# The last rows of a matmul with row normalization: a square moved from ScalarE to VectorE, and scalings moved to GpSimd

## The chip, the core and the metric

The kernel runs on one core of a Trainium2 chip. The metric is the device time of one execution in microseconds (us). A profiled execution leaves a trace as well: start and duration of every instruction on TensorE (PE), VectorE (DVE), ScalarE (ACT) and GpSimd (POOL), and the issues and landings of the transfers that SyncE's queue (SP) starts.

## The reference

```python
x = np.matmul(a, b)                                   # 2048 x 2048 by 2048 x 2048, fp32
rms = np.sqrt(np.mean(x ** 2, axis=-1, keepdims=True) + eps)
return (gamma * x / rms).astype(np.float32)           # gamma: one value per column
```

A row can be written only when the squares of all of its 2048 columns are summed. What follows that sum is one factor r = 1/rms per row, which is a column of 128 values, one per partition, for a block of 128 rows.

## The kernel before

The output has 16 blocks of 128 rows. Blocks are worked on in pairs (`g`), and each pair in two halves of 1024 columns (`j`), by a Strassen-like scheme of seven products on 512-column chunks: `do(n, m)` issues the eight matmuls of product `m` of half `n` (`product`, line 363, matmul at line 358), and the chunks x11, x12, x21, x22 are put together from PSUM banks by additions on VectorE (`add`, line 101) and copies on ScalarE. In a half, x11 and x12 are the 512-column chunks of the pair's first block, x21 and x22 those of its second. The kernel writes every engine's order by hand: each engine runs its instructions in the order of the program's text, and waits come from the dependences alone.

The change lies in the last function, `last_group`, which finishes the last pair of blocks: `ra` is block 14, `rb` is block 15. For `rb`, four chunks of 512 columns are squared and summed into the columns of a small tile `msq[rb]` (`square_of`, line 272, an ACT Square whose accumulator output is the sum). The steps that the prediction speaks of are these.

- Line 814: ACT copies the bank of the last product 7 to x21[1].
- Lines 818 to 822 scale three chunks of block 14 by its factor `r_a`: ACT the left one (`by_r`, line 754), POOL the chunk `mid` (line 820), DVE x11[1] (line 822). The fourth, x12[1], gets gamma and `r_a` in one DVE instruction (`scaled_gamma`, line 750, called at line 826). SP writes them out in three transfers (lines 819, 821, 827: 256, 256 and 512 KB).
- Lines 823 to 825: DVE adds the x21[1] of line 814 to two half banks of 256 columns each, and to x22[1].
- Line 828 is the last full product. Its result is the left chunk of block 15; ACT squares it (line 829) straight from PSUM, then squares x22[1] (line 830), and DVE multiplies the left chunk by gamma (line 831).
- Lines 832 and 845: two small DVE instructions put together `part`, the sum of all squares of block 15 but for those of the very last 256 columns.
- Lines 837 to 846: the last product goes in two halves of 256 columns (matmuls at line 839), each squared by ACT (line 842). Between the two, DVE makes `part` and multiplies the chunk x22[1] by gamma (line 846).
- Line 847: ACT takes the root (line 288), DVE the reciprocal `r_b` (line 293).
- Lines 848 to 854 scale block 15: DVE the left chunk (line 848), then SP writes it (line 849, 256 KB); ACT chunks 1 and 3 (line 851, recorded as line 754), DVE chunk 2 in two halves with gamma (line 853, recorded as line 750). SP's last transfer (line 854, 768 KB) waits for all three.

Of the kernel before, what the change touches and what calls it, by code (L numbers as in the profile page):

```python
# [8 lines left out]
FP32 = mybir.dt.float32  # L9
# [4 lines left out]
ALU = mybir.AluOpType  # L14
# [3 lines left out]
def kernel(  # L18
# [13 lines left out]
    nc = tc.nc  # L32
    P = 128
# [6 lines left out]
    CH = 512  # L40
# [13 lines left out]
    stat_pool = ctx.enter_context(tc.tile_pool(name="stat_pool", bufs=4))  # L54
# [3 lines left out]
    inv_sqrt_n = 1.0 / float(N) ** 0.5  # L58
# [41 lines left out]
    def add(out, in0, in1, op=ALU.add):  # L100
        nc.vector.tensor_tensor(out=out, in0=in0, in1=in1, op=op)  # L101
# [104 lines left out]
    msq = {}  # L206
# [53 lines left out]
    def x_tile(mb, h):  # L260
        if (mb, h) not in x_half:
            x_half[mb, h] = x_slot[slot_of[mb, h]]
        return x_half[mb, h]

    def x_chunk(mb, c):
        return x_tile(mb, c // 2)[:, (c % 2) * CH:(c % 2 + 1) * CH]

    def square_of(mb, src):
        c = n_sq[mb]
        n_sq[mb] += 1  # L270
        sq = sq_pool.tile([P, 2 * CH], BF16, name="sq")
        nc.scalar.activation(out=sq[:, 0:src.shape[-1]], in_=src, func=ACTF.Square,  # L272
                             scale=inv_sqrt_n, accum_out=msq[mb][:, c:c + 1])

    def square_half(mb, h):
        square_of(mb, x_tile(mb, h))
# [4 lines left out]
    def take_pre(mb):  # L281

        pre_of[mb] = stat_pool.tile([P, 1], FP32, name="pre")
        add(pre_of[mb], msq[mb][:, 0:1], msq[mb][:, 1:2])
# [11 lines left out]
    def square_right(mb):  # L296

        square_half(mb, 1)
        rms_of[mb] = root(msq[mb][:, 2:3], pre_of.pop(mb))

    def rows(mb, lo, hi):
        return out[mb * P:(mb + 1) * P, lo:hi]
# [207 lines left out]
    x11, x12, x21, x22 = (x_chunk(r, c) for r in (r2, r3) for c in (2, 3))  # L510
# [45 lines left out]
    def chunks(n):  # L556
        g, j = halves[n]
        return [x_chunk(2 * g + r, 2 * j + c) for r in range(2) for c in range(2)]

    def do(n, m, copies=True):  # L560

        if n >= len(halves) or n < 0:
            return
        g, j = halves[n]
        b1, b2, b3 = B1[n % 2], B2[n % 2], B3[n % 2]
        if g >= G2:
            b1 = b2
        product(g, j, m, {1: b1, 2: b1, 3: b3, 4: b2, 5: b3, 6: b2, 7: B7}[m],
                start=m in (1, 7))
        if m == 1 and g >= G2:  # L570
            nc.scalar.copy(out=chunks(n)[0], in_=b2)
        elif m == 1:
            nc.scalar.copy(out=b2, in_=b1)  # L573
        elif m == 6:
            nc.scalar.copy(out=b3, in_=b2)  # L575
        elif m == 7 and copies:
            nc.scalar.copy(out=chunks(n)[2], in_=B7)  # L577
# [44 lines left out]
    def first_sums(n):  # L622

        return [chunks(m)[0] for m in (n - 2, n - 1, n, n + 1)]
# [115 lines left out]
    def last_group():  # L740
        n = len(halves) - 2
        g = NG - 1
        ra, rb = 2 * g, 2 * g + 1
        x11, x12, x21, x22 = zip(chunks(n), chunks(n + 1))
        xa, xb = x_tile(ra, 0), x_tile(rb, 0)
        gam = [gamma_sb[:, c * CH:(c + 1) * CH] for c in range(NCH)]
        gam_left = gamma_sb[:, 0:HALF]

        def scaled_gamma(x, src, r, gamma_of_x):
            nc.vector.scalar_tensor_tensor(out=x, in0=src, scalar=r, in1=gamma_of_x,  # L750
                                           op0=ALU.mult, op1=ALU.mult)

        def by_r(x, r):
            nc.scalar.activation(out=x, in_=x, func=ACTF.Copy, scale=r)

        b2, b3 = [B2[(n + j) % 2] for j in range(2)], [B3[(n + j) % 2] for j in range(2)]
        x00, x01 = first_sums(n)[0:2]
        do(n, 6)
        step(g - 1, 1, X2)
        nc.scalar.copy(out=W2, in_=X2)  # L760
        square_right(rb - 2)
        do(n - 1, 3)
        step(g - 1, 2, W2)
        step(g - 1, 6, X2)
        nc.scalar.copy(out=Y2, in_=X2)
        finish(rb - 2)
        take(n - 1, 12)
        add(x00, W2, x00)
        do(n + 1, 1)
        step(g - 1, 5, Y2)  # L770
        step(g - 1, 7, W2)
        step(g - 1, 4, X2)
        square_half(ra - 2, 0)
        add(x11[1], Y2, x11[1])
        a_sums(g, (4,))
        add(x11[0], W2, x11[0])
        add(x11[1], W2, x11[1])
        take_pre(ra - 2)
        square_of(ra, x11[1])
        do(n, 5)  # L780
        nc.scalar.copy(out=x22[0], in_=b3[0])
        add(x11[0], X2, x11[0])
        step(g - 1, 3, Y2)
        add(x01, Y2, x01)
        square_right(ra - 2)
        do(n + 1, 6)
        finish(ra - 2)
        do(n, 7)
        add(x22[0], x21[0], x22[0])
        add(b2[0], b2[0], x21[0])  # L790
        square_of(rb, x22[0])
        add(x11[1], x11[1], gam[2], ALU.mult)
        do(n + 1, 5)
        nc.scalar.copy(out=x22[1], in_=b3[1])
        wide = a_pool.tile([P, K], FP32, name="a32")
        chunk = [wide[:, c * CH:(c + 1) * CH] for c in range(NCH)]
        add(chunk[1], x22[0], gam[1], ALU.mult)
        pre_b = stat_pool.tile([P, 1], FP32, name="part")
        add(pre_b, msq[rb][:, 0:1], msq[rb][:, 1:2])
        do(n, 3)  # L800
        take(n, 12)
        square_half(ra, 0)
        pre_a = stat_pool.tile([P, 1], FP32, name="pre")
        nc.vector.tensor_scalar(out=pre_a, in0=msq[ra][:, 0:1], scalar1=msq[ra][:, 1:2],
                                scalar2=msq[ra][:, 2:3], op0=ALU.add, op1=ALU.add)
        add(xa, xa, gam_left, ALU.mult)
        do(n + 1, 3)
        take(n + 1, 12)
        square_of(ra, x12[1])
        rms_a = root(msq[ra][:, 3:4], pre_a)  # L810
        r_a = inverse(rms_a)
        other = X2
        product(g, 1, 7, other)
        nc.scalar.copy(out=x21[1], in_=other)
        halves2 = [slice(0, CH // 2), slice(CH // 2, CH)]
        half = [bank[:, 0:CH // 2] for bank in (B1[1], b3[0])]
        left, mid = xa[:, 0:CH], xa[:, CH:]
        by_r(left, r_a)
        nc.sync.dma_start(out=rows(ra, 0, CH), in_=left)
        nc.gpsimd.tensor_scalar_mul(out=mid, in0=mid, scalar1=r_a)  # L820
        nc.sync.dma_start(out=rows(ra, CH, HALF), in_=mid)
        nc.vector.tensor_scalar_mul(out=x11[1], in0=x11[1], scalar1=r_a)
        for bank, col in zip(half, halves2):
            add(bank, b2[1][:, col], x21[1][:, col])
        add(x22[1], x21[1], x22[1])
        scaled_gamma(x12[1], x12[1], r_a, gam[3])
        nc.sync.dma_start(out=rows(ra, HALF, N), in_=x_tile(ra, 1))
        do(n, 4)
        square_of(rb, b2[0])
        square_of(rb, x22[1])  # L830
        add(xb[:, 0:CH], b2[0], gam[0], ALU.mult)
        nc.vector.tensor_scalar(out=pre_b, in0=pre_b, scalar1=msq[rb][:, 2:3],
                                scalar2=msq[rb][:, 3:4], op0=ALU.add, op1=ALU.add)

        half_sq = stat_pool.tile([P, 2], FP32, name="n2")
        part = stat_pool.tile([P, 1], FP32, name="part")
        for h, (bank, col) in enumerate(zip(half, halves2)):
            for kp in range(KP):
                nc.tensor.matmul(bank, quarter(g, 1, 1)[:, kp, :], sums[1][:, 2, kp, col],
                                 start=False, stop=(kp == KP - 1), skip_group_check=True)  # L840
            sq = sq_pool.tile([P, 2 * CH], BF16, name="sq")
            nc.scalar.activation(out=sq[:, 0:CH // 2], in_=bank, func=ACTF.Square,
                                 scale=inv_sqrt_n, accum_out=half_sq[:, h:h + 1])
            if h == 0:
                add(part, half_sq[:, 0:1], pre_b)
                add(chunk[3], x22[1], gam[3], ALU.mult)
        r_b = inverse(root(half_sq[:, 1:2], part))
        nc.vector.tensor_scalar_mul(out=xb[:, 0:CH], in0=xb[:, 0:CH], scalar1=r_b)
        nc.sync.dma_start(out=rows(rb, 0, CH), in_=xb[:, 0:CH])
        for c in (1, 3):  # L850
            by_r(chunk[c], r_b)
        for bank, col in zip(half, halves2):
            scaled_gamma(chunk[2][:, col], bank, r_b, gam[2][:, col])
        nc.sync.dma_start(out=rows(rb, CH, N), in_=wide[:, CH:])

    first_segment()
# [37 lines left out]
```

## Time and profile before

| | us |
|---|---|
| median of three runs | 220.34 |
| lowest and highest of them | 219.80, 221.61 |
| the profiled execution, its own time | 219.88 |
| its span in the trace | 218.10 |
| PE busy in the span | 207.6 (95%) |
| DVE busy | 161.9 (74%) |
| ACT busy | 113.6 (52%) |
| POOL busy | 36.8 (17%) |
| last matmul issued, its start | 210.85 |
| last transfer issued | 213.83 |

The profiled execution took 1.78 us more than its span and lies 0.46 us below the median of the three runs. A line of the timeline gives start, duration, engine, line of the program, operation, and output and inputs with their shapes. An idle time before an instruction and what ended it stand in square brackets. SPq is the queue from which SyncE issues transfers.

### The profile page before, as it was taken

The page shows a single profiled execution, that of the slowest core. Times are in us where ns is not written, and L with a number is a line of the kernel's source. Part 1 is how long each engine was busy: PE and PEld are TensorE (multiplying, and loading weights), DVE is VectorE, ACT ScalarE, POOL GpSimd, SP SyncE. Part 2 cuts the span into 40 slices and gives each one's busy share as a digit, 9 for nine tenths or more (in the row PEclk, how much of TensorE's full clock was granted, in tenths as well). Part 3 has the DMA queues.
Part 4 walks back from the last instruction along what each step waited for, and adds up shares of the span by engine and source line. Part 5 has one row for each costly group of instructions (what it writes and reads, how often), then busy time and mean ns, then how long its engine had stood idle before and what let it go on. Part 6 is the DMA issues. An engine that isn't in the chain of part 4 may idle for free.

```text
span 218.1 us, 2969 instructions
## 1 busy us (share of the span) xinstructions
PE 207.6 (95%) x1004; PEld 97.1 (45%) x1024; DVE 161.9 (74%) x327; ACT 113.6 (52%) x225; POOL 36.8 (17%) x73
## 2 busy tenths in 40 slices
PE   7899999999999999999999999999999999999970
PEld 3444544444455444444444444444444444444440
DVE  1128769999999974989985899399856984485781
ACT  2110002900598565889726962594728951555782
POOL 7544444334001000300021001100101000000030
PEclk9999999999999999999999999999999999999996
DMA  7999999999949888599774995497595993040454
GB/s 153 171 201 207 203 206 209 212 207 221 408 171 377 304 228 238 150 345 283 237 227 168 345 277 100 183 243 241 126 273 215 316 256 72 0 192 3 192 187 198
DMA packets 37039, 46.60 MB, mean 214 GB/s; under 512 B 22560, under 2 KB 26656, under 8 KB 35744
## 3 DMA queue, kind: packets, MB, share of 16 engines
q0 software_dynamic: 10608, 23.86, 45.3%
q1 hardware_dynamic: 26144, 22.29, 34.8%
q10 hardware_dynamic: 272, 0.26, 0.3%
q8 instruction: 8, 0.13, 0.2%
q14 instruction: 7, 0.06, 0.1%
HBM read 34.60 MB, written 16.78 MB: 236 GB/s over the span
## 4 chain that ended last, share of the span: by engine, by line
PE 80%; DMA 6%; ACT 6%; DVE 4%; issue 2%; POOL 1%; ACTq 0%; another core or an unknown queue 0%; SPq 0%; POOLq 0%
PE acc L358 53%; PE acc L406 16%; PE acc L397 3%; DMA early<-in_a_dram 3%; DMA out_dram<-x 3%; ACT sq L272 2%; PE tbank L397 2%; PE tbank L432 2%; DVE x L311 2%; PE tbank L182 2%; PE tbank L358 1%; DVE x L101 1%; ACT acc L573 0%; PE tbank L195 0%; POOL b L115 0%
## 5 line engine op out<-in xcount | busy, mean ns | idle before, releaser
L358 PEld LDWEIGHTS <-s 128*128 128x128 f16 (+1 forms) x312 | 30.4, 98 | 37.5 <-DVE s L335 1.1
L272 ACT ACTIVATE sq<-x 128x1024 bf16<-128x1024 f32 (+1 forms) x33 | 33.2, 1005 | 25.0 <-DVE x L101 21.1
L406 PE MATMUL acc<-b,head_at 128*128 128x512 bf16 x171 | 42.3, 379 | 0.6 <-DMA b<-in_b_dram 0.4
L311 DVE SCALAR_TENSOR_TENSOR x<-x,r,gamma_sb 128x1024 f32<-128x1024 f32 x28 | 34.9, 1282 | 0.5
L358 PE MATMUL acc<-b,head_at 128*128 128x512 bf16 x133 | 33.6, 379 | 0.2
L101 DVE TENSOR_TENSOR x<-acc,x 128x512 f32<-128x512 f32 x33 | 22.2, 687 | 10.7 <-PE acc L397 4.7
L358 PEld LDWEIGHTS <-head_at 128*128 128x128 f16 (+1 forms) x184 | 17.9, 98 | 21.0
L358 PE MATMUL acc<-b,at_even 128*128 128x512 bf16 x110 | 26.2, 379 | 0.2
L406 PEld LDWEIGHTS <-head_at 128*128 128x128 bf16 x176 | 16.9, 97 | 19.7 <-issue 0.7
L358 PE MATMUL acc<-early,s 128*128 128x512 bf16 x102 | 25.4, 379 | 0.2
L358 PE MATMUL acc<-b,s 128*128 128x512 bf16 x100 | 24.3, 379 | 0.2
L358 PEld LDWEIGHTS <-at_even 128*128 128x128 f16 x160 | 15.7, 98 | 18.9
L224 ACT ACTIVATE sq<-a 128x1024 bf16<-128x1024 f32 x22 | 23.3, 1058 | 0.5
L358 PE MATMUL acc<-t_left,s 128*128 128x512 bf16 x95 | 22.5, 379 | 0.1
L115 POOL DMA_DIRECT2D b<-in_b_dram x32 | 17.2, 541 | 20.5 <-DMA b<-in_b_dram 14.1
L442 ACT COPY x<-acc 128x512 f32<-128x512 f32 x7 | 4.1, 580 | 25.6 <-PE acc L406 25.6
L575 ACT COPY acc<-acc 128x512 f32<-128x512 f32 x12 | 6.9, 575 | 10.6 <-PE acc L358 10.6
L293 DVE RECIPROCAL r<-rms 128x1 f32<-128x1 f32 x16 | 2.6, 160 | 12.1 <-ACT rms L288 12.0
L187 DVE COPY head_at<-tbank 128x1024 bf16<-128x1024 bf16 x7 | 4.8, 692 | 8.3 <-PE tbank L182 8.3
L820 POOL TENSOR_SCALAR x<-x,r 128x512 f32<-128x512 f32 x1 | 1.9, 1855 | 42.0 <-DVE r L293 42.0
L101 DVE TENSOR_TENSOR x<-tbank,x 128x512 f32<-128x512 f32 x9 | 6.2, 689 | 3.6 <-PE tbank L432 3.6
L577 ACT COPY x<-acc 128x512 f32<-128x512 f32 x10 | 5.8, 585 | 5.0 <-PE acc L358 5.0
(133 smaller groups left out, 244.7 us busy)
## 6 DMA issues: line engine op xcount, KB each, us to landing
out_dram<-x SPq DMA_DIRECT2D x29, 512.0 KB, 3.7
a<-in_a_dram POOLq DMA_DIRECT2D x9, 1024.0 KB, 5.9
b<-in_b_dram POOLq DMA_DIRECT2D x32, 256.0 KB, 9.9
a<-in_a_dram POOLq DMA_DIRECT2D x4, 512.0 KB, 9.8
early<-in_a_dram POOLq DMA_DIRECT2D x7, 256.0 KB, 10.0
gamma_sb<-in_gamma_dram POOLq DMA_DIRECT2D x2, 512.0 KB, 9.9
head_at<-in_a_dram POOLq DMA_DIRECT2D x1, 1024.0 KB, 8.9
out_dram<-x SPq DMA_DIRECT2D x3, 256.0 KB, 2.6
```

The lines of the kernel that those rows point to most:

```text
L101: nc.vector.tensor_tensor(out=out, in0=in0, in1=in1, op=op)
L115: nc.gpsimd.dma_start(out=raw[j][kp][:, t, :], in_=b[lo:lo + P, j * HALF:(j + 1) * HALF])
L182: nc.tensor.matmul(view[:, t, r, :], ah(kp)[:, r, t * P:(t + 1) * P], identity, is_transpose=True, start=(t == 0 and r == 0), stop=(t == 1 ...
L187: nc.vector.tensor_copy(out=head_at[:, 2 * kp:2 * kp + 2, :, :], in_=view)
L224: nc.scalar.activation(out=junk, in_=a32[mb][:, h * HALF:(h + 1) * HALF], func=ACTF.Square, scale=2.0 ** -8, accum_out=n2[:, h:h + 1])
L272: nc.scalar.activation(out=sq[:, 0:src.shape[-1]], in_=src, func=ACTF.Square, scale=inv_sqrt_n, accum_out=msq[mb][:, c:c + 1])
L311: nc.vector.scalar_tensor_tensor(out=x, in0=x, scalar=inverse_of[mb], in1=gamma_sb[:, h * HALF:(h + 1) * HALF], op0=ALU.mult, op1=ALU.mult)
L358: nc.tensor.matmul(bank, lhsT[:, kp, :], rhs, start=(start and kp == 0), stop=(kp == KP - 1), skip_group_check=not start)
L397: nc.tensor.matmul(bank, lhsT[:, k, :], rhs, start=(m in (1, 7) and k == 0), stop=(k == KQ - 1), skip_group_check=m not in (1, 7))
L406: nc.tensor.matmul(bank, head_at[:, kt, r, :], head_rhs(c, kt), start=(kt == 0), stop=(kt == KT - 1))
L575: nc.scalar.copy(out=b3, in_=b2)
L577: nc.scalar.copy(out=chunks(n)[2], in_=B7)
```

## The change

VectorE computes the squares of x22[1] and their sum itself, in one `tensor_tensor_reduce` that writes the squares into the not yet used `chunk[3]` and starts its sum from `pre_b`; it stands before the scaling of x12[1]. The ACT square of x22[1] and the small DVE instruction of line 832 are gone, and `part` is made by one instruction with three summands. In block 14, x11[1] is scaled by GpSimd instead of VectorE, behind `mid`. In block 15, ACT scales the left chunk (before: VectorE), GpSimd chunk 1 (before: ACT), and chunk 3 is shared, its first 256 columns by ACT and its last 256 by GpSimd (before: all by ACT, 512 columns). Every scaling on GpSimd is now a `tensor_scalar` with two multiplications, by r and by 1.0.

```diff
+        def by_r_pool(x, r):
+            nc.gpsimd.tensor_scalar(out=x, in0=x, scalar1=r, scalar2=1.0,
+                                    op0=ALU.mult, op1=ALU.mult)
+
         by_r(left, r_a)
         nc.sync.dma_start(out=rows(ra, 0, CH), in_=left)
-        nc.gpsimd.tensor_scalar_mul(out=mid, in0=mid, scalar1=r_a)
+        by_r_pool(mid, r_a)
         nc.sync.dma_start(out=rows(ra, CH, HALF), in_=mid)
-        nc.vector.tensor_scalar_mul(out=x11[1], in0=x11[1], scalar1=r_a)
+        by_r_pool(x11[1], r_a)
         for bank, col in zip(half, halves2):
             add(bank, b2[1][:, col], x21[1][:, col])
         add(x22[1], x21[1], x22[1])
+        sum_b = stat_pool.tile([P, 1], FP32, name="sum_b")
+        nc.vector.tensor_tensor_reduce(out=chunk[3], in0=x22[1], in1=x22[1],
+                                       scale=inv_sqrt_n * inv_sqrt_n, scalar=pre_b,
+                                       op0=ALU.mult, op1=ALU.add, accum_out=sum_b)
         scaled_gamma(x12[1], x12[1], r_a, gam[3])
         nc.sync.dma_start(out=rows(ra, HALF, N), in_=x_tile(ra, 1))
         do(n, 4)
         square_of(rb, b2[0])
-        square_of(rb, x22[1])
         add(xb[:, 0:CH], b2[0], gam[0], ALU.mult)
-        nc.vector.tensor_scalar(out=pre_b, in0=pre_b, scalar1=msq[rb][:, 2:3],
-                                scalar2=msq[rb][:, 3:4], op0=ALU.add, op1=ALU.add)
...
             if h == 0:
-                add(part, half_sq[:, 0:1], pre_b)
+                nc.vector.tensor_scalar(out=part, in0=half_sq[:, 0:1], scalar1=msq[rb][:, 2:3],
+                                        scalar2=sum_b, op0=ALU.add, op1=ALU.add)
                 add(chunk[3], x22[1], gam[3], ALU.mult)
         r_b = inverse(root(half_sq[:, 1:2], part))
-        nc.vector.tensor_scalar_mul(out=xb[:, 0:CH], in0=xb[:, 0:CH], scalar1=r_b)
+        by_r(xb[:, 0:CH], r_b)
         nc.sync.dma_start(out=rows(rb, 0, CH), in_=xb[:, 0:CH])
-        for c in (1, 3):
-            by_r(chunk[c], r_b)
+        by_r_pool(chunk[1], r_b)
         for bank, col in zip(half, halves2):
             scaled_gamma(chunk[2][:, col], bank, r_b, gam[2][:, col])
+        by_r(chunk[3][:, halves2[0]], r_b)
+        by_r_pool(chunk[3][:, halves2[1]], r_b)
         nc.sync.dma_start(out=rows(rb, CH, N), in_=wide[:, CH:])
```

## The prediction

> **What bounds the kernel now.** I read the page first: PE is busy for 95% of the span, but all edits lie behind line 818, and the last matmul starts at 210.85 of 218.1 us. So only the tail counts. There the chain that ended last runs (ACT copy 207.68, ACT by_r, a wait for the product of line 828 until 209.41, four ACT squares, root, reciprocal, two ACT scalings, the last transfer). Then I read the timeline of the last 11 us, engine by engine.
>
> ```profile
> 207.68 0.59 ACT L814 COPY x<-tbank 128x512 f32<-128x512 f32 x1
> 207.86 0.49 DVE L822 TENSOR_SCALAR x<-x,r 128x512 f32<-128x512 f32 x1
> 207.92 1.85 POOL L820 TENSOR_SCALAR x<-x,r 128x512 f32<-128x512 f32 x1 [42.02 <-DVE r L293]
> 208.30 0.76 DVE L101 TENSOR_TENSOR acc<-acc,x 128x256 f32<-128x256 f32 x2
> 208.97 0.68 DVE L101 TENSOR_TENSOR x<-x 128x512 f32<-128x512 f32 x1
> 209.57 0.75 DVE L750 SCALAR_TENSOR_TENSOR x<-x,r,gamma_sb 128x512 f32<-128x512 f32 x1
> 210.13 0.63 ACT L272 ACTIVATE sq<-x 128x512 bf16<-128x512 f32 x1
> 210.24 0.68 DVE L101 TENSOR_TENSOR x<-acc,gamma_sb 128x512 f32<-128x512 f32 x1
> 210.88 0.38 ACT L842 ACTIVATE sq<-acc 128x256 bf16<-128x256 f32 x1
> 210.89 0.27 DVE L832 TENSOR_SCALAR part<-part,msq 128x1 f32<-128x1 f32 x1
> 211.39 0.38 ACT L842 ACTIVATE sq<-acc 128x256 bf16<-128x256 f32 x1
> 211.39 0.16 DVE L101 TENSOR_TENSOR part<-n,part 128x1 f32<-128x1 f32 x1 [0.23 <-ACT sq L842]
> 211.47 0.68 DVE L101 TENSOR_TENSOR a<-x,gamma_sb 128x512 f32<-128x512 f32 x1
> 211.90 0.30 ACT L288 ACTIVATE rms<-n,part 128x1 f32<-128x1 f32 x1
> 212.23 0.16 DVE L293 RECIPROCAL r<-rms 128x1 f32<-128x1 f32 x1
> 212.43 0.49 DVE L848 TENSOR_SCALAR x<-x,r 128x512 f32<-128x512 f32 x1
> 212.47 1.33 ACT L754 ACTIVATE a<-a,r 128x512 f32<-128x512 f32 x2 [0.28 <-DVE r L293]
> 212.94 0.33 SPq L849 DMA_DIRECT2D out_dram<-x  x1
> 213.83 0.33 SPq L854 DMA_DIRECT2D out_dram<-a  x1
> ```
>
> The reader is to see two things. ACT sets r_b: its squares follow one another without a gap until the root at 211.90. But DVE is only just behind: it waited 0.23 us before `part`, and the multiplication of line 846 ended at 211.47 + 0.68 = 212.15, 0.08 before the reciprocal of 212.23. DVE has some 0.3 us of slack in this stretch, no more.
>
> Two more views. One is POOL beside DVE at line 146, where POOL copies a single column; the other is the list of transfers, with the median from issue to landing as its last number.
>
> ```profile
> 87.58 1.25 POOL L146 CAST pace<-head_at 128x1 f32<-128x1 f16 x1 [19.55 <-DMA head_at<-a]
> ...
> 87.50 2.48 DVE L311 SCALAR_TENSOR_TENSOR x<-x,r,gamma_sb 128x1024 f32<-128x1024 f32 x2
> ...
> 164.82 0.19 POOL L146 COPY pace<-a 128x1 f32<-128x1 f32 x1 [7.24 <-DMA a<-in_a_dram]
> ```
>
> ```profile
> out_dram<-x SPq DMA_DIRECT2D x3, 256.0 KB, 2.6
> out_dram<-a SPq DMA_DIRECT2D x1, 768.0 KB, 3.3
> ```
>
> The POOL copy of one column takes 0.19 us beside an idle DVE, and a POOL cast of one column took 1.25 us when it began during a two-input DVE instruction: it ended at 88.83, where the first of the two DVE instructions ended (87.50 + 1.24 = 88.74). So a POOL row contains time in which POOL only waited for DVE.
>
> **The change part by part.**
>
> *ScalarE loses the square of line 830* (210.13 to 210.86, with its accumulator read: 0.75 us). This isn't gained in full, for PE is late next. The last matmul runs 210.85 to 211.12; from the last matmul of line 828 (ends about 209.2) to the ACT square that needs it (209.41) passed 0.2 us, so the last square can start at 211.32 instead of 211.39. Gain on this path: 0.07 us. By ACT alone, r_b would start at 212.16.
>
> *VectorE loses line 822, gains the squares.* Line 822 (0.49) goes, but the next DVE instruction, the two bank additions, needs ACT's copy, which ends at 208.27; they start at 208.30 now and will then. Removing line 822 gives nothing; its cover is that wait. The new instruction has no row. From below it is bounded by a plain two-input instruction of this size (0.68), from above by one that passes the elements twice (1.28, the 1024-column row of line 311). I take 0.80: the row of line 750 (0.75) is nearest, with two inputs and a scalar, and an accumulator must come out as well. It needs the x22 just written: a dependent DVE instruction starts 0.04 after the end of the one before (reciprocal 207.66 + 0.16, next 207.86), an independent one 0.08 ahead of it. So: squares 209.69 to 210.49; line 826 from 210.41; line 831 from 211.08 (step 0.67 as now); the new `part` from 211.73 (step 0.65), 0.27 long like line 832; line 846 from 211.92 (a one-column `tensor_scalar` took a step of 0.19 before the next: 205.88, 206.07) to 212.60; reciprocal from 212.52. The root is no later: part ends at 212.00, root by 212.34. Before, the reciprocal started at 212.23, so r_b comes 0.29 us later. Queued behind the new instruction are all of those, and what waits for r_b. Bounds: with 0.68 it is 0.17, with 1.28 it is 0.77 later. Below zero is ruled out: even the lower bound is more than the slack.
>
> *Block 14 on POOL.* POOL `mid` starts at 207.92, now beside an idle DVE; the multiplication of x11[1] queues behind it and behind nothing else. The transfer of line 827 waits for it and for line 826, which ends at 210.41 + 0.75 = 211.16 instead of 210.32. It is issued at 211.2 to 211.7 instead of 210.35, and its data (the DMA engines became busy 0.7 us after line 819's issue; about 1.3 us long) are through by about 213.7, just as the next transfer starts. SP's order keeps line 849 behind 827, which is issued well before. So nothing on the path; without that cover it costs the overlap with line 849, up to 0.3 us.
>
> *What a POOL scaling costs.* Above: 1.85 us for 512 columns as recorded. Below: copy of one column 0.19, and the page's 128-column POOL select is 0.29, a slope of 0.85 ns per column, so 0.19 + 0.44 = 0.62. I take 0.62, and 0.40 for 256 columns: line 820 began beside line 822 (until 208.35) and ran beside the two-input x22 addition (208.97 to 209.65); 1.85 less those 0.43 and 0.68 leaves 0.74, which is nearer to 0.62. Behind r_b, DVE reads one input from PSUM, so POOL runs free there. Whether two multiplications cost more or less than one, no row shows; the same ends hold it.
>
> The SBUF page of the Trainium skill ("SBUF — State Buffer", section "Who interferes with whom") says that a two-input VectorE instruction and a reading GpSimd instruction exclude each other, and that the first to start holds the port for its whole length. The cast above agrees; line 820, which should have held up the x22 addition at 208.97 and did not (0.68, as ever), does not. By the page, x11[1] on POOL would hold up the x22 addition by the rest of its length, from 208.97 to about 209.2, 0.2 us more at the end; by the row, by nothing.
>
> "GPSIMD Engine Reference", section 3.1, speaks against the change: it calls GpSimd's loop slower than VectorE's and gives 769 ns for 512 elements in its best case. By that the last POOL work would take 1.15 us in place of my 1.02, and the last issue would be 0.1 us later.
>
> *After r_b* (ends 212.69): ACT scales the left chunk in 0.72 from 212.76 (0.07 behind r_b as now) to 213.48; line 849 is issued at 213.50, 0.56 later than now (212.94). Then ACT does 256 columns: the step between two such scalings is 0.61, and 0.72 less 0.25 (the difference of the 512- and 256-column squares) gives 0.47, so 213.37 to 213.84. POOL: 0.10 behind r_b (as at 207.92), 0.62 + 0.40, done at 213.81. DVE chunk 2 takes 0.87 and is done by 213.65. The last issue is at 213.87, 0.04 later than now.
>
> *The end.* From the last issue alone: +0.04. But the two transfers, 1024 KB, share the engines: 256 KB land in 2.6 us, 512 KB in 3.1, so each 256 KB takes 0.5 behind a fixed 2.1; from line 849's issue all four quarters need 4.1, and 212.94 + 4.1 = 217.04 is where the last one landed (213.83 + 3.3 = 217.13). By that the end follows the issue of line 849: +0.56. Both fit the one case that the trace has; I take +0.4, nearer to the second, as the DMA engines are 81% busy from 214.6 to 217.
>
> **Sum:** 219.88 + 0.4 = 220.3 on the profiled execution's scale. That execution lies 0.46 below the median 220.34; on the median's scale it is 220.7.
>
> **The rivals.**
>
> *POOL is as slow as its row (1.85).* For: the only such row. Against: the DVE rows beside it. Then 1.85 and 1.02 (half of the slope) behind 212.79 end at 215.66, the last issue is at 215.69, +1.9: 222.2. It decides as soon as the two POOL scalings together exceed 1.05 us.
>
> *POOL holds up VectorE.* If the port is held through, the x22 addition and the squares wait for x11[1], once or twice 0.5 us, straight into r_b, since DVE has no slack left: +1.1, so 221.4. For it: POOL does wait for DVE in the casts. Against it: no DVE row of the tail is lengthened.
>
> *VectorE isn't the bound* (other side). If the squares pass nearly beside their neighbours (a step below 0.35), r_b follows PE, 0.07 earlier; the last issue is then at 213.51, 0.32 earlier, and with the end following it the time is 220.0. For: DVE starts independent instructions 0.08 early. Against: no row of 512 fp32 columns with two inputs has a step below 0.60.
>
> **How the numbers follow.** Forecast 0.60 (220.0 to 221.3, from the ends +0.04 and +0.8 and the spread of runs); slow POOL 0.17; held VectorE 0.13; VectorE not the bound 0.10. The range of eight in ten, 219.6 to 222.3, leaves out the tails of the first and last case. About 1% is what a measurement can tell here, 2.2 us: above 222.54 lies less than half of the slow POOL case and a little of the held one, 0.10; below 218.14 almost nothing, 0.04, for what I haven't seen; within, 0.86.
>
> **What would show it.** Right: no ACT square at 210.13 and the first half's square at about 210.3; a DVE row of 0.7 to 0.9 us behind the x22 addition; the reciprocal of r_b right behind line 846's multiplication, with no idle time, at about 212.5; POOL rows of 0.6 and 0.4 us behind r_b; line 849 issued 0.6 later, line 854 about 0.1. Wrong: the reciprocal waiting for the root; POOL rows above 1 us; two-input DVE rows above 0.75; a last landing that follows line 854 alone.

## The result, and the profile after

Over 22 runs of each kernel the median went from 220.56 to 221.81 us. The ratio of the times is 1.006, with a 95% interval of 1.0033 to 1.0087: the change costs about 1.3 us (0.7 to 1.9). The profiled execution took 221.77 us, its span is 220.0, against 219.88 and 218.1 before.

Of the 1.9 us between the two spans, 0.59 lie ahead of everything that was edited: block 14's reciprocal starts at 208.25 instead of 207.66. In the runs below, whose code up to there is the same, it starts anywhere from 207.39 to 208.89, so this part is chance. From here on, times are counted from the start of block 14's reciprocal; then two traces can be laid over each other, and the end is at 10.43 before (218.08 - 207.66) and at 11.75 after (219.99 - 208.25). The 1.32 us between them agree with the 1.3 of the medians.

The timeline of the tail after the change, answering to the lines shown of before (start, duration, engine, line; some lines have new numbers, and the operation CUSTOM_DVE_ANT_0 of line 832 is the new `tensor_tensor_reduce`):

```profile
208.51 1.36 POOL L820 TENSOR_SCALAR x<-x,r 128x512 f32<-128x512 f32 x2 [41.81 <-DVE r L293]
...
209.56 0.86 DVE L101 TENSOR_TENSOR x<-x 128x512 f32<-128x512 f32 x1
...
210.46 0.75 DVE L832 CUSTOM_DVE_ANT_0 a<-x,part 128x512 f32<-128x512 f32 x1
...
210.93 0.38 ACT L848 ACTIVATE sq<-acc 128x256 bf16<-128x256 f32 x1 [0.25 <-PE acc L845]
211.13 0.08 DVE L832 DVE_READ_ACCUMULATOR2_ANT sum_b<- 128x1 f32 x1
...
211.81 0.38 ACT L848 ACTIVATE sq<-acc 128x256 bf16<-128x256 f32 x1 [0.40 <-PE acc L845]
...
212.40 0.27 DVE L851 TENSOR_SCALAR part<-n,msq,sum_b 128x1 f32<-128x1 f32 x1
212.58 0.68 DVE L101 TENSOR_TENSOR a<-x,gamma_sb 128x512 f32<-128x512 f32 x1
212.76 0.29 ACT L288 ACTIVATE rms<-n,part 128x1 f32<-128x1 f32 x1 [0.48 <-DVE part L851]
213.18 0.16 DVE L293 RECIPROCAL r<-rms 128x1 f32<-128x1 f32 x1
...
213.49 1.15 POOL L820 TENSOR_SCALAR a<-a,r 128x512 f32<-128x512 f32 x2 [3.61 <-issue]
...
214.12 0.33 SPq L856 DMA_DIRECT2D out_dram<-x  x1
214.66 0.33 SPq L862 DMA_DIRECT2D out_dram<-a  x1
```

ACT, whose squares ran without a gap up to the root before, now waits for PE ahead of both half-bank squares (0.25 and 0.40 us), and 0.48 us for DVE's `part` ahead of the root. DVE, which has no idle time from the x22 addition to the reciprocal, has become the bound of r_b. The x22 addition took 0.86 instead of 0.68 beside GpSimd's second scaling. Counted from block 14's reciprocal, r_b's reciprocal starts at 4.93 instead of 4.57, the left chunk goes out at 5.87 instead of 5.28 and the last transfer at 6.42 instead of 6.18. The last landing is at 10.05 instead of 9.46, 0.59 later.

That is less than half of the loss. The rest lies behind the last landing. The instructions at the program's end, from the views of line 889 (before) and line 897 (after); the columns are the number of instructions, their shortest, median and longest duration in ns, and their first and last start:

```profile
L889 POOLq DRAIN  x3: 46/93/6499, 207.9 to 217.8; - x3
L889 SPq DRAIN  x3: 7/7/7, 217.3 to 217.6; - x3
```

```profile
L897 POOLq DRAIN  x3: 46/93/5727, 213.5 to 219.7; - x3
L897 SPq DRAIN  x3: 7/7/7, 218.4 to 219.5; - x3
```

Each engine's queue ends with a drain, and then all of them meet. GpSimd's first drain is the long one. Before, it starts at 207.86 and lasts 6.50, so it ends at 214.36, while SyncE, having seen the last landing, comes to the meeting at 217.3: nobody waits for GpSimd. After, it starts at 213.49 and ends at 219.22, while SyncE is there at 218.44. Everyone waits 0.78 us for GpSimd. (From the last landing to the end it is 1.70 us instead of 0.97, so 0.73 longer; with the 0.59 this is the whole 1.32.) In both traces the drain ends 4.58 us after GpSimd's last instruction (209.78 and 214.64). The waits of SyncE's queue show the same from the other side, as a wait for the other engines at the end, before and after:

```profile
SPq L889 <- PEq L889: 0.7, 2, 0.5
```

```profile
SPq L897 <- PEq L897: 1.4, 2, 0.9
```

The columns are the wait in all, how often, and the longest. The name PEq is of little use here (several engines are waited for, and PE had long been done); the drain's row tells which it was.

### The profile page after: what moved, and what is told of

It reads as the page before. It is cut to its first block, busy times and chain, and to the rows that moved or that the text cites. A ratio compares the mean times of both kernels' runs of the same rounds, so it can differ in the third digit from the quotient of the medians.

```text
span 220.0 us, 2990 instructions
## 1 busy us (share of the span) xinstructions
PE 208.3 (95%) x1024; PEld 96.5 (44%) x1024; DVE 161.8 (74%) x326; ACT 112.8 (51%) x223; POOL 36.6 (17%) x76
## 4 chain that ended last, share of the span: by engine, by line
PE 71%; DMA 10%; DVE 6%; ACT 5%; issue 3%; POOL 1%; POOLq 0%; SPq 0%; DVEq 0%; ACTq 0%
PE acc L358 47%; PE acc L406 16%; DMA early<-in_a_dram 3%; DMA out_dram<-x 3%; DVE x L311 2%; DMA a<-in_a_dram 2%; ACT sq L272 2%; PE acc L397 2%; PE tbank L432 2%; DMA head_at<-a 2%; PE tbank L182 2%; PE tbank L397 1%; ACT sq L224 1%; DVE x L101 1%; PE tbank L358 1%
## 5 line engine op out<-in xcount | busy, mean ns | idle before, releaser
L272 ACT ACTIVATE sq<-x 128x1024 bf16<-128x1024 f32 (+1 forms) x32 | 32.5, 1016 | 23.5 <-DVE x L101 20.7
L406 PE MATMUL acc<-b,head_at 128*128 128x512 bf16 x176 | 43.0, 379 | 1.1 <-DMA b<-in_b_dram 1.1
L358 PE MATMUL acc<-b,head_at 128*128 128x512 bf16 x136 | 33.9, 379 | 0.0
L820 POOL TENSOR_SCALAR x<-x,r 128x512 f32<-128x512 f32 x2 | 1.4, 685 | 41.8 <-DVE r L293 41.8
```

The source lines that it names most:

```text
L358: nc.tensor.matmul(bank, lhsT[:, kp, :], rhs, start=(start and kp == 0), stop=(kp == KP - 1), skip_group_check=not start)
L406: nc.tensor.matmul(bank, head_at[:, kt, r, :], head_rhs(c, kt), start=(kt == 0), stop=(kt == KT - 1))
```

## The experiments

The theory: three things cost time, each by itself. The squares on VectorE make r_b later; GpSimd's scaling of x11[1] holds up VectorE's x22 addition, and so r_b; and GpSimd's work behind r_b puts its drain, 4.58 us behind its last instruction, past the last landing. The rival: the end follows the writes alone, the first of which now waits for ScalarE, and what lies behind the last landing is chance.

**The changed kernel without GpSimd behind r_b.**

```diff
-        by_r(xb[:, 0:CH], r_b)
+        nc.vector.tensor_scalar_mul(out=xb[:, 0:CH], in0=xb[:, 0:CH], scalar1=r_b)
...
-        by_r_pool(chunk[1], r_b)
+        for c in (1, 3):
+            by_r(chunk[c], r_b)
...
-        by_r(chunk[3][:, halves2[0]], r_b)
-        by_r_pool(chunk[3][:, halves2[1]], r_b)
```

> The changed kernel with block 15 scaled as before (VectorE the left chunk, ScalarE chunks 1 and 3), so that GpSimd's last instruction is the scaling of x11[1] in block 14. All times are counted from the start of block 14's reciprocal r_a; before: r_b at 4.57, last landing 9.46, end 10.43; after: r_b 4.93, last landing 10.05, end 11.75. Drain theory (GpSimd's closing drain ends 4.58 us after its last instruction in both traces, and the end waits for it): GpSimd is done early, the lag from the last landing to the end falls back from 1.70 to 0.97; r_b stays at 4.93 by VectorE's order, so the end is at 10.43 + 0.36 = 10.8, 0.9 us less than after, 0.4 us over before. Rival, writes alone: the end follows the issue of the left chunk's transfer and the exit lag is chance: lag anywhere between 0.97 and 1.7, end 10.8 to 11.5.

Measured: r_b at 4.93, last landing 9.82, end 10.79; ratio to before 1.0034 (0.9998 to 1.007). The lag from the last landing to the end is 0.97, as before. The part behind r_b thus costs 0.96 of the 1.32 us.

**The kernel before with only the new scalings of block 15**, the same edit the other way round.

> The kernel before with only the new scalings of block 15 (ScalarE the left chunk and half of chunk 3, GpSimd chunk 1 and the other half by two multiplications). r_b stays at 4.57 as before. Drain theory: GpSimd ends at about 4.57 + 0.17 + 0.10 + 0.69 + 0.47 = 6.0, its drain ends 4.58 later at 10.6, 0.9 us behind the signal of SyncE before (9.61), so the end is at 11.3 to 11.4, 0.9 us slower than before. Rival, writes alone: the left chunk's transfer goes out 0.25 later and the last one 0.2 earlier: end 10.3 to 10.7, no more than 0.3 us slower.

Measured: r_b 4.57, last landing 9.69, end 11.40; ratio 1.0044 (1.0015 to 1.0072). GpSimd's last instruction ends at 6.04 and its drain at 10.62. The writes alone would have cost 0.23.

**The kernel before with one late GpSimd instruction that does nothing useful.**

```diff
             scaled_gamma(chunk[2][:, col], bank, r_b, gam[2][:, col])
+        wait_for(chunk[2][:, CH - 1:CH])
```

`wait_for(src)` is the kernel's own helper, `nc.gpsimd.tensor_copy(out=pace, in_=src)`, at line 146; nothing behind it reads `pace`.

> The kernel before with one more GpSimd instruction: a copy of a single column that waits for VectorE's last scaling of block 15 (ends at 6.04) and that nobody waits for. Drain theory: it ends at about 6.3, the drain 4.58 later at 10.9, the end at 11.6, 1.2 us slower than before with unchanged work and unchanged writes. Rival: nothing depends on it, so 10.43 and no change; a part of 1.2 would say that the drain depends on the kind or the size of the last instruction.

Measured: end 11.72, 1.29 later than before, with every issue and landing where it was (last landing 9.47); ratio 1.0068 (1.0035 to 1.01). This is the cleanest of the runs. From its timeline of GpSimd and the view of its last line:

```profile
213.80 0.18 POOL L146 COPY pace<-a 128x1 f32<-128x1 f32 x1 [4.05 <-DVE a L750]
```

```profile
L890 POOLq DRAIN  x3: 46/102/4776, 213.8 to 219.1; - x3
L890 SPq DRAIN  x3: 7/7/13, 217.2 to 218.8; - x3
```

The copy of one column is over at 213.98; the drain that began at 213.79 lasts 4.78 us, to 218.56, while SyncE stands ready at 217.2. A fifth of a microsecond of work that nobody waits for costs as much as the whole change.

**The same with a memset of r_b's 128 values in place of the copy**, one execution.

```diff
+        nc.gpsimd.memset(r_b, 0.0)
```

> The kernel before with a GpSimd memset of the 128 values of r_b at the very end, once their readers are done (about 6.1). It only writes, where the one-column copy reads and writes. If every late GpSimd instruction starts the 4.58 us of the drain anew: drain ends near 10.8, end 11.5. If only instructions that read do: 10.43, as before.

Measured: the memset takes 0.10 and ends at 6.31; drain to 10.89, end 11.68. It doesn't matter here that it only writes.

**The same with a copy of r_b as soon as it is there**, one execution.

```diff
         r_b = inverse(root(half_sq[:, 1:2], part))
+        wait_for(r_b)
```

> The kernel before with a GpSimd copy of the one column r_b as soon as it is there (4.74 from block 14's reciprocal). Drain theory as a maximum of two ends: the copy ends at about 5.0, the drain at 9.6, and SyncE's signal comes at 9.61: end 10.4 to 10.5, no change, though GpSimd works 2.9 us later than before. Rival, any GpSimd instruction behind r_b costs time: an end of 10.8 or more.

Measured: end 10.66, neither of the two. The copy was expected to end at 5.0; it took 0.43 and ended at 5.29, and it lay beside VectorE's scaling of the left chunk:

```profile
212.20 0.49 DVE L849 TENSOR_SCALAR x<-x,r 128x512 f32<-128x512 f32 x1
...
212.30 0.43 POOL L146 COPY pace<-r 128x1 f32<-128x1 f32 x1 [2.74 <-DVE r L293]
```

Then 4.58 more is 9.87, 0.26 behind SyncE's 9.61, and the end is 0.23 later. The mechanism held; the size of the copy was wrong. That it waited for VectorE is likely, not shown by a run of its own: it ended 0.04 behind that scaling, and a GpSimd scaling that began beside the same VectorE operation in block 14 was 0.29 longer than one alone (0.98 against 0.69, in a run below). The limit for GpSimd's last instruction in this kernel is thus at 9.61 - 4.58 = 5.03, only 0.3 us behind r_b.

**The changed kernel with GpSimd scaling by one multiplication.**

```diff
-            nc.gpsimd.tensor_scalar(out=x, in0=x, scalar1=r, scalar2=1.0,
-                                    op0=ALU.mult, op1=ALU.mult)
+            nc.gpsimd.tensor_scalar_mul(out=x, in0=x, scalar1=r)
```

> The changed kernel with each GpSimd scaling by one multiplication instead of two, all else equal. If a GpSimd row of 1.85 us (before) was waiting for VectorE and not work, the two rows behind r_b, beside a VectorE that reads PSUM, stay at 0.69 and 0.48 and the time is that of after. If the form with one multiplication is the slow one, those rows are about 1.85 and 1.0, GpSimd ends 1.7 us later, the drain ends 1.7 us later, and the kernel is 1.7 us slower than after (3 us over before).

Measured: end 13.19, 1.44 later than after the change (1.7 expected), ratio 1.0138 (1.0083 to 1.0192). The groups of GpSimd in the tail, first with one multiplication, then with two (the changed kernel); the columns are busy us, mean ns of one, and the idle time before:

```profile
L820 POOL TENSOR_SCALAR x<-x,r 128x512 f32<-128x512 f32 x2 | 3.2, 1584 | 42.3 <-DVE r L293 42.3
L820 POOL TENSOR_SCALAR a<-a,r 128x512 f32<-128x512 f32 x1 | 1.6, 1563 | 1.9 <-issue 1.9
L820 POOL TENSOR_SCALAR a<-a,r 128x256 f32<-128x256 f32 x1 | 0.9, 923 | 0.0
```

```profile
L820 POOL TENSOR_SCALAR x<-x,r 128x512 f32<-128x512 f32 x2 | 1.4, 685 | 41.8 <-DVE r L293 41.8
L820 POOL TENSOR_SCALAR a<-a,r 128x512 f32<-128x512 f32 x1 | 0.7, 692 | 3.6 <-issue 3.6
L820 POOL TENSOR_SCALAR a<-a,r 128x256 f32<-128x256 f32 x1 | 0.5, 479 | 0.0
```

The second multiplication, by 1.0, makes the instruction more than twice as fast: 0.69 instead of 1.56 us. Of the 1.85 in the trace of before, only some 0.3 was waiting for VectorE (1.85 - 1.56).

**The changed kernel with the square back on ScalarE**, and with it the two small additions of before.

```diff
-        sum_b = stat_pool.tile([P, 1], FP32, name="sum_b")
-        nc.vector.tensor_tensor_reduce(out=chunk[3], in0=x22[1], in1=x22[1],
...
         square_of(rb, b2[0])
+        square_of(rb, x22[1])
...
```

> The changed kernel with the square of x22[1] back on ScalarE and the two small additions of before, all GpSimd scalings kept. Times count from block 14's reciprocal. VectorE-order theory: the new instruction on VectorE is what moved r_b from 4.57 to 4.93, so r_b is back at 4.57 to 4.6; the end is then set by GpSimd's drain as in the run that has the new end alone: 11.4, 0.35 less than after and 1.0 over before. Rival (GpSimd's lock on the x22 addition moved r_b): r_b stays near 4.75 and the end near 11.6.

Measured: r_b 4.57, end 11.40; ratio 1.0031 (0.9991 to 1.0072), which alone would not tell the two theories apart; the trace does. The x22 addition still took 0.86, but VectorE's idle time swallowed it.

**The changed kernel, block 15 scaled as before, x11[1] on VectorE again**: of the change only the squares and `mid` are left.

```diff
-        by_r_pool(x11[1], r_a)
+        nc.vector.tensor_scalar_mul(out=x11[1], in0=x11[1], scalar1=r_a)
...
```

> The changed kernel with block 15 scaled as before and x11[1] of block 14 scaled by VectorE again, so that GpSimd has only the first chunk. The x22 addition took 0.86 instead of 0.68 when GpSimd's second scaling lay beside it. Lock theory: without it 0.68 again, r_b at 4.93 - 0.18 = 4.75, end 10.6. If the addition's 0.86 has another cause: r_b stays at 4.93, end 10.8. GpSimd's one scaling starts beside VectorE's scaling and takes about 1.0 to 1.1 (0.69 and a wait of up to 0.43).

Measured: r_b 4.75, end 10.60; ratio 1.0013 (0.9972 to 1.0054). The x22 addition is at 0.68 again, and GpSimd's one scaling, beside VectorE's, took 0.98. From its timeline of VectorE, beside that of the run without GpSimd behind r_b, which differs in x11[1] alone:

```profile
208.84 0.68 DVE L101 TENSOR_TENSOR x<-x 128x512 f32<-128x512 f32 x1
209.56 0.75 DVE L832 CUSTOM_DVE_ANT_0 a<-x,part 128x512 f32<-128x512 f32 x1
```

```profile
208.96 0.86 DVE L101 TENSOR_TENSOR x<-x 128x512 f32<-128x512 f32 x1
209.86 0.75 DVE L832 CUSTOM_DVE_ANT_0 a<-x,part 128x512 f32<-128x512 f32 x1
```

In the second, GpSimd's scaling of x11[1] ended at 209.28 and the addition at 209.82. The section "Who interferes with whom" of the Trainium skill's "SBUF — State Buffer", that the instruction which started first holds the port, fits in kind: 0.18 of delay. It doesn't fit in size. Held until 209.28, the whole addition of 0.68 would have ended at 209.96, a delay of 0.32; the last section has rows that don't fit at all.

**The kernel before with block 14's part alone**: the two scalings of `by_r_pool` in place of lines 820 and 822, all else as before.

> The kernel before with only block 14's part of the change: two chunks on GpSimd by two multiplications, VectorE's scaling of x11[1] gone; squares and block 15 as before. GpSimd ends at 1.63, its drain at 6.2, far ahead of the end. The x22 addition is held up by 0.18, which VectorE's idle 0.23 before part takes up; r_b at 4.57, end 10.4, no change against before. If the lock reaches r_b: 4.65 to 4.75 and an end of 10.5 to 10.6.

Measured: r_b 4.57, end 10.43; ratio 1.0005 (0.9967 to 1.0044). Without the squares behind it, the delay of the addition vanishes in VectorE's slack.

**A try at a faster write-out**: the kernel before with block 15 in four transfers.

```diff
-        nc.vector.tensor_scalar_mul(out=xb[:, 0:CH], in0=xb[:, 0:CH], scalar1=r_b)
-        nc.sync.dma_start(out=rows(rb, 0, CH), in_=xb[:, 0:CH])
+        for h, col in enumerate(halves2):
+            nc.vector.tensor_scalar_mul(out=xb[:, col], in0=xb[:, col], scalar1=r_b)
+            nc.sync.dma_start(out=rows(rb, h * CH // 2, (h + 1) * CH // 2), in_=xb[:, col])
         for c in (1, 3):
             by_r(chunk[c], r_b)
+            if c == 1:
+                nc.sync.dma_start(out=rows(rb, CH, 2 * CH), in_=chunk[1])
...
-        nc.sync.dma_start(out=rows(rb, CH, N), in_=wide[:, CH:])
+        nc.sync.dma_start(out=rows(rb, 2 * CH, N), in_=wide[:, 2 * CH:])
```

> The kernel before with block 15 written in four transfers instead of two: the left chunk in halves, each scaled by VectorE and sent by itself (128 KB), chunk 1 by itself, chunks 2 and 3 together. In before, after and the runs with one part of the change, the last landing came 4.18 after the left chunk's issue. If the bytes behind the first issue set the end, the first issue is 0.13 earlier and the landing at 9.33, end 10.3. If the last issue or the number of transfers sets it: VectorE's chunk 2 ends 0.15 later, the landing stays at 9.45 to 9.7, end 10.4 to 10.7.

Measured: last issue 6.55, last landing 9.69, end 11.04; ratio 1.0023 (0.9987 to 1.0059). The second expectation holds for the landing: 9.69, 3.14 after the last of four issues, which came 0.37 later than before; whether it was this issue or the number of transfers wasn't parted. The end went beyond both. SyncE came to the meeting 0.51 after the last landing, where it was 0.14 to 0.15 in the other runs. The trace tells why: at the end SyncE waits for the transfers' semaphores (the marks that a transfer has landed) one after another in a fixed order, some 0.06 us each. In the other eleven traces one such wait is left behind that of the last transfer; in the trace of before 0.13 us pass from there to SyncE's drain. Here the last transfer has another semaphore, with seven waits behind it, and 0.49 us pass. Without these 0.37 more the end would be at 10.67, an estimate that lies inside the second expectation; no run tried it. No version in this study beats the kernel before.

All of them in one table, us from the start of block 14's reciprocal, from the traces. "SyncE ready" is the drain with which SyncE comes to the meeting, "drain ends" GpSimd's long one.

| kernel | r_b | left chunk issued | last landing | SyncE ready | drain ends | end |
|---|---|---|---|---|---|---|
| before | 4.57 | 5.28 | 9.46 | 9.61 | 6.71 | 10.43 |
| after | 4.93 | 5.87 | 10.05 | 10.20 | 10.97 | 11.75 |
| no GpSimd behind r_b | 4.93 | 5.64 | 9.82 | 9.96 | 6.22 | 10.79 |
| new end alone | 4.57 | 5.51 | 9.69 | 9.83 | 10.62 | 11.40 |
| late copy | 4.57 | 5.28 | 9.47 | 9.61 | 10.94 | 11.72 |
| late memset | 4.57 | 5.28 | 9.46 | 9.61 | 10.89 | 11.68 |
| copy at r_b | 4.57 | 5.28 | 9.46 | 9.61 | 9.87 | 10.66 |
| one multiplication | 5.07 | 6.00 | 11.10 | 11.24 | 12.42 | 13.19 |
| square on ScalarE | 4.57 | 5.51 | 9.68 | 9.83 | 10.61 | 11.40 |
| squares and `mid` alone | 4.75 | 5.46 | 9.64 | 9.78 | 5.83 | 10.60 |
| block 14 alone | 4.57 | 5.29 | 9.46 | 9.61 | 6.22 | 10.43 |
| four transfers | 4.57 | 5.15 | 9.69 | 10.20 | 6.70 | 11.04 |

In every row the end comes 0.77 to 0.84 after the later of "SyncE ready" and "drain ends". Added in this order, the parts of the change cost 0.17 for the squares with `mid` (10.60 - 10.43), 0.19 for x11[1] on GpSimd (10.79 - 10.60) and 0.96 for the end of block 15 (11.75 - 10.79), of which 0.23 are the later first write and 0.73 the drain. So the theory was wrong in "each by itself": GpSimd's scaling of x11[1] costs something only once the squares have used up VectorE's slack, and nothing without them. The end of block 15 costs the same in the kernel before (0.97, 11.40 - 10.43). The rival fails on the late copy, where no write moved and the end came 1.29 later.

## Why the prediction was right, and where it was not

The time, 221.81, lies in the range of eight in ten (219.6 to 222.3) and within the 1% given 0.86. The likeliest case was too low: +0.4 was forecast, +1.3 came, above its own range of 220.0 to 221.3. That the wider range held is in part luck. Its upper part was there for a slow GpSimd and a held VectorE; the first didn't come in the new form, the second came with a sixth of its price, and more than half of the loss is the drain, which no case had.

*ScalarE loses a square, and it isn't gained.* Right; PE is late next, as said. The half-bank squares started at 2.68 and 3.56 (before: 3.22 and 3.73); the last one gained 0.17 where 0.07 was expected, and ACT then waited for DVE.

*VectorE loses line 822, gains the squares.* The mechanism was right, and removing line 822 gave nothing, as said. The slip of 0.29 was too large for this part alone: the squares by themselves moved r_b by 0.18, and the lower bound (0.17) was nearer. Half of the difference is the new instruction, 0.75 instead of 0.80; the other half is the step from line 831 to `part`, 0.60 instead of 0.65. The measured slip of 0.36 is the 0.18 plus a step which the forecast had put at nothing:

*POOL holds up VectorE.* The forecast followed line 820 of before, beside which the x22 addition ran undisturbed, against the page's rule, from which it had worked out 0.2. The addition was held up by 0.18. That the two figures are so close is in part chance, since by that rule and the measured rows it would be 0.32. As a rival the same mechanism was priced at 1.1, six times too much. A two-input VectorE row above 0.75 was one of the prediction's own signs of being wrong, and it came (0.86).

*What a POOL scaling costs.* The value was close (0.62 and 0.40, measured 0.69 and 0.48), the reason false. The prediction took 1.85 for 0.7 of work and 1.1 of waiting; with one multiplication it was 1.56 of work. The slow POOL of the first rival was real for the old form, and the second multiplication took it away. 0.69 is also below the 769 ns that section 3.1 of the Trainium skill's "GPSIMD Engine Reference" gives for 512 elements in its best case.

*After r_b.* The left chunk's issue moved by 0.59, close to the 0.56 of the forecast, but by errors that cancel: r_b came 0.36 later instead of 0.29, ACT in DVE's place cost 0.23 instead of 0.27, and the 0.36 itself is squares priced too high and a held addition priced at nothing. The last issue came 0.24 later where 0.04 had been worked out: 0.07 by r_b and the rest by GpSimd's longer scalings.

*The end.* The second of the two readings was right: the last landing came 4.17 to 4.19 after the left chunk's issue in ten of the twelve traces, all but those with one multiplication and with four transfers. It moved by 0.59, where 0.56 had been worked out and 0.4 was taken.

*The step that failed* is the sum: 219.88 + 0.4 took what lies behind the last landing for a constant (0.97 us before). It is the later of two ends, and the prediction priced GpSimd's work behind r_b up to the last issue only. The rows for it were in the trace of before: the drain of 6.50 us, 4.58 of them behind line 820's end, was over 2.90 us before SyncE was ready. GpSimd's last instruction moved from 2.12 to 6.39, by 4.27 us, so that margin was gone: the drain ended 0.78 us after SyncE was ready, and the end came 1.70 behind the last landing in place of 0.97.

## What to carry to other kernels

An engine that is idle at the end isn't always free: look in the trace for what its queue still does behind its last instruction, and count the new last instruction from there to the end. Here GpSimd may work until 4.58 us before SyncE is ready, and each microsecond past that is one on the total. Work taken off an engine (here ACT's square of 0.75 us) gains only what the next wait leaves: here 0.17 us until PE was late, and then nothing, as DVE was later still. And parts of a change are best run one by one in one trace each, counted from a common event, where medians with an interval of a third of a per cent either way can't part them.

## What the runs showed of the hardware

GpSimd's drain at the program's end finished 4.58 us after its last instruction in all twelve traces, whether that was a scaling of 512 or 256 columns, a copy of one column or a memset; what it waits for isn't known, and a transfer issued by GpSimd as its last instruction wasn't tried. A GpSimd `tensor_scalar` over 512 fp32 columns took 0.69 us with two multiplications and 1.56 with one. VectorE's `tensor_tensor_reduce` of 512 columns took 0.75 with two equal inputs, and reading its sum 0.08 more, beside the next instruction. Beside a GpSimd scaling with one multiplication the x22 addition wasn't held up (0.68, before and in the run with one multiplication), though a GpSimd scaling that had begun first was still running; but in the latter the squares behind it took 1.06; which part of such a GpSimd instruction holds VectorE up stays open. SyncE's closing waits, for transfers that had landed, took some 0.06 us each.
